# An encoder block with 32 experts: two more weight slots, sums over experts kept in PSUM, down biases added later, conditional loads on another queue

## The chip, the cores and the metric

The kernel runs on one core of a Trainium2 chip, as one launch. Times are device microseconds of that core. The kernel before ran three times: 1157.16, 1157.80 and 1158.95 us, median 1157.8 us. A further execution was taken with the profiler; its rows are what is read below.

## The reference, cut to what matters

One layer of an encoder over 256 tokens of width 1024, in float32. Two attention mixers (one that picks 64 keys per token with an indexer, one over chunks with a position bias) read one combined projection of x, are merged under gates, and are followed by a normalisation. Then comes a mixture of experts, and a second normalisation. Nearly all the data is in the experts: 32 of them, each with three matrices of 1024 x 1024.

```
x = layer_norm(DN_ALPHA * x + merged @ w_out, ln1_g, ln1_b)
logits = x @ w_router + b_router           # top 4 of 32, softmax over the four
for each expert e, for the tokens that take it:
    hg = min(xb @ w_gate[e] + b_gate[e], 7)
    hu = clip(xb @ w_up[e] + b_up[e], -7, 7)
    h  = (hu + 1) * hg * sigmoid(1.702 * hg)
    y  = (h @ w_down[e] + b_down[e]) * gate
ffn = sum over experts
x = layer_norm(DN_ALPHA * x + ffn, ln2_g, ln2_b)
```

## The kernel before, in words

**Slots.** Large data lies in a pool of NSLOT = 25 buffers ("slots") of 128 partitions x 8 KiB, 1 MiB each. All matrices are cut into chunks of one slot. `plan` puts them into one list in the order of their use: 24 chunks of the attention's matrices, then per expert eight chunks of gate and up and four of down, with gate and up of the next expert ahead of down of this one. `load_next` (line 83) takes the next chunk of the list into a slot; `pump(reserve)` repeats that while fewer than NSLOT - reserve slots are in use, counted as the program is written out. A load whose slot is still being read waits on its queue until the reader is done. `done` and `free` give slots back to the count. In the first stage `used()` calls `pump` with the reserves of the list RESERVE, 25 numbers written out by hand, so that slots remain for the halves into which ACT, DVE and POOL split the matrices (lines 175 and 180).

**Order.** The schedule is by hand: each engine and each queue runs its instructions in the order in which the program writes them. SP's queue issues the loads. It also issues the small ones, in the program's order: router weights and position bias (lines 392 to 394), x and the first norm's vectors (657, 658), gate and up biases (882, 883), down biases (900).

**Experts.** From about 221 us the loop over experts runs. For expert e, PE multiplies the gathered tokens (64 rows at most) with gate and up (`gate_up`, lines 759 and 761), ACT copies the products out of PSUM, then PE does the down product of expert e-1 (`down`, 793). At odd e it gathers the tokens of the next pair of experts by products with one-hot matrices (`dispatch`, 635) and turns the gates (744). Then `act_fn` turns the products of gate and up (776), and DVE and ACT compute h. At even e `combine` (808) spreads a pair's rows over the 256 tokens, into PSUM banks c0 and c1, and DVE adds these to the sum `acc`, a slot in SBUF (814). `acc` begins as ALPHA times x1 at expert 0.

**PSUM.** All tiles in PSUM come from one pool of eight banks (`bank`), reused as they are released. At the last expert four banks are opened as `sums`: eight instructions multiply `acc` with the identity into them (963), and the last pair's rows are added there (990), from where the second norm reads them.

**Down biases.** At expert 3 `down_biases` loads the 32 x 1024 table into a slot (900), multiplies it with the turned gates (908), and DVE adds the four results to `acc` (910). It also computes the largest count of tokens of an expert, `cnti`. The slot is kept until expert 20.

**Overflow.** At expert 20 `overflow` reads `cnti` into a register on each engine (831) and branches (832): if an expert has more than 64 tokens, a loop over all experts works off the rest, with loads by SP inside the block. With the inputs here the block is not run. The loads that `pump` issues after expert 19's down weights, in the call with e = 19, go out on POOL's queue in place of SP's.

Of the kernel before, what the change touches and what calls it, by code (L numbers as in the profile page):

```python
# [15 lines left out]
NT = 2  # L16
# [4 lines left out]
CAP = 64  # L21
TOPK = 64
# [6 lines left out]
NSLOT = 25  # L29
# [19 lines left out]
def body(nc, tc, slots, sm, psp, xT_d, x_d, w_g0, w_qi, w_in, ikgb_d, wuk_d,  # L49
# [4 lines left out]
    # ---------------------------------------------------------------- slots and loads  # L54
# [53 lines left out]
    def plan_d(e):  # L108
        if e < NE - 1:
            for c in range(4):  # L110
                plan(("d", e, c), wd_d[e, c])
            return
        # the last expert's by halves of the columns
        for c2 in range(2):
            for h in range(2):
                plan(("dl", h, c2), lambda t, h=h, c2=c2: [
                    (t[:, i * 1024:(i + 1) * 1024].rearrange("p (k f) -> p k f", k=2),
                     wd_d[e, 2 * c2 + i].rearrange("p (k f) -> p k f", k=2)[:, :, h * 512:(h + 1) * 512])
                    for i in range(2)])
# [7 lines left out]
    # ---------------------------------------------------------------- first loads  # L127
# [13 lines left out]
    # ---------------------------------------------------------------- constants and small loads  # L141
    ident = sm.tile([128, 128], F32, name="ident")
    make_identity(nc, ident)
    ikgb = sm.tile([128, 3], F32, name="ikgb")
    SP.dma_start(ikgb, ikgb_d)
# [9 lines left out]
    epst = sm.tile([128, 1], F32, name="epst")  # L155
# [14 lines left out]
    # ---------------------------------------------------------------- exact halves of float32 operands  # L170
# [6 lines left out]
    def split(t, hi, lo, rnd=acopy, sub=G):  # L177
        """hi = t rounded to float32r, lo = what is left of it"""
        rnd(hi.bitcast(F32R), t)
        sub.tensor_tensor(lo.bitcast(F32R), t, hi, op=ALU.subtract)  # L180

    # the matrices whose products run on halves, in the order of their use
# [4 lines left out]
    def ahead(n):  # L187
        """splits the first n chunks of that order"""
        for key in order[len(halves):n]:
            t = take(key)  # L190
            hi, lo = slot("hi"), slot("lo")
            sub = {"V": V, "G": G}[LO_ENGINE[len(halves)]]
            for h in range(2):
                cs = slice(h * 1024, (h + 1) * 1024)
                split(t[:, cs], hi[:, cs], lo[:, cs], sub=sub)
            halves.append((hi, lo))
            done(1)

    def part(i, which, k, per):
        """row block k of chunk i"""  # L200
        return halves[i][which].bitcast(F32R).rearrange("p (k c) -> p k c", k=per)[:, k, :]
# [5 lines left out]
    def used():  # L207
        """chunk done with"""
        free(2)
        pump(next(pumps))  # L210

    # ---------------------------------------------------------------- index queries, feature-major
# [6 lines left out]
    def warm(n):  # L219
        """keeps the tensor engine's clock up while it waits"""  # L220
        p = bank("warm")
        for _ in range(n):
            PE.matmul(p[:, 0:128], wt, wt, start=True, stop=True)
# [31 lines left out]
    def project(g, sink):  # L255
        """group g of the input projections, token-major"""
        ps = [bank("tm") for _ in range(NT)]
        for c in range(2):
            i = IN + 2 * g + c
            ahead(i + 1 + AHEAD[i])  # L260
            for tb in range(NT):
                for k in range(4):
                    for a, b in THREE:
                        PE.matmul(ps[tb], xHL[a][:, 4 * c + k, tb * 128:(tb + 1) * 128], part(i, b, k, 4),
                                  start=(c + k + a + b == 0), stop=(c == 1 and k == 3 and b == 1))
                if c == 1:
                    sink(tb, ps[tb])
            used()

    def project_T(g, sink):  # L270
        """group g of the input projections, feature-major; two row blocks share a bank, so only the first starts it"""
# [21 lines left out]
    # k_idx layer norm and c_kv rms norm, token-major  # L293
# [26 lines left out]
    def head_scores(qT, kT, tb, sink):  # L320
        """pairs of heads lie on the two halves of the partitions"""
# [14 lines left out]
    # ---------------------------------------------------------------- B queries and keys, the indexer  # L336
# [51 lines left out]
    # ---------------------------------------------------------------- A queries  # L388
# [8 lines left out]
    # ---------------------------------------------------------------- attention  # L397
# [91 lines left out]
    # ---------------------------------------------------------------- merge  # L489
# [21 lines left out]
    def branch(w, c, ps):  # L511
        """chunk c of a branch's rows; at the last one the gate and, for B, the sum of the two and its halves"""
# [36 lines left out]
    def norm_apply(tb, groups):  # L549
        """z = (x1 - mean) * rstd, and x1 = z * g + b"""  # L550
# [38 lines left out]
    def route_sums(copy=vcopy):  # L589
        """the router's products by experts, in four sums over two row blocks each"""  # L590
        p = bank("rt")
        for k in range(KD):
            g = k % 4
            PE.matmul(p[32 * g:32 * g + 32, 0:128], wrg[:, k, :], zT[:, k, :], start=(k < 4), stop=(k >= 4),
                      skip_group_check=True)
        copy(rsum, p[:, 0:128])

    def route(tb):
        """the router's logits (the norm's gain in the weights, its offset in the row), and which experts a token takes"""
# [9 lines left out]
    def count_up(tb):  # L609
        """the place of each token among an expert's tokens; far off for the tokens that it doesn't take"""  # L610
# [11 lines left out]
    sgm = wa_s[:, 1536:1792].rearrange("p (j s) -> p j s", j=4)  # L622

# [38 lines left out]
    # the second token tile's last columns in two halves, for a shorter way from their sums to the norm  # L662
# [66 lines left out]
    # ---------------------------------------------------------------- experts  # L729
# [9 lines left out]
    def combine_weights(pt, gated):  # L739
        """pt = the gated one-hot rows turned, from their two halves of 64 columns for each token tile"""  # L740
# [6 lines left out]
    def dispatch_weights(g):  # L747
        """for the pair g of experts"""
# [39 lines left out]
    def down(hT, wd):  # L788
        """the halves of the columns on the halves of the partitions"""
# [7 lines left out]
    def rows_of(e, p, first=0, size=512):  # L797
        """an expert's rows to its half of the pair's partitions"""
        r = slice(64 * (e % 2), 64 * (e % 2) + 64)
        for n in range(2):  # L800
            acopy(work["y"][r, first + n * size:first + (n + 1) * size], p[64 * n:64 * n + 64, 0:size])

    def combine(g):
        """adds a pair's rows to the sums"""
        for tb in range(NT):
            ps = [bank("c0"), bank("c1")]
            for n in range(2):
                PE.matmul(ps[n], work["pt"][:, g % 2, tb, :], work["y"][:, n * 512:(n + 1) * 512], start=True, stop=True)  # L808
            add(tb, ps)

    def add(tb, ps):
        for n in range(2):
            cs = slice(n * 512, (n + 1) * 512)
            V.tensor_tensor(acc[:, tb, cs], acc[:, tb, cs], ps[n], op=ALU.add)
# [8 lines left out]
    def overflow(s):  # L823
# [8 lines left out]
        with tc.If(rv > CAP):  # L832
            for r in range(1, T // CAP):
                with tc.For_i(0, NE, 1) as e:
# [18 lines left out]
                    def stream(src):  # L853
                        def get(j, cs):
                            o = (j % 2) * 1024
                            SP.dma_start(ow, src[col, j // 2, :, o + cs.start:o + cs.stop]
# [9 lines left out]
                    for tb in range(NT):  # L866
                        cps = [bank("c0"), bank("c1")]
                        for n in range(2):
                            h = slice(64 * n, 64 * n + 64)
                            PE.matmul(cps[n], opt[h, tb, :], y[h, :], start=True, stop=True)  # L870
                        add(tb, cps)
# [23 lines left out]
    def down_biases():  # L895
        """the gates' share of the down biases; the largest count of an expert's tokens"""
        bd_s = slot("bd")
        gT = bd_s[0:NE, 1024:1024 + T]
        bd = bd_s[0:NE, 0:1024]
        SP.dma_start(bd, bd_d)  # L900
# [4 lines left out]
        for tb in range(NT):  # L905
            for n in range(2):
                p = bank("bd")
                PE.matmul(p, gT[:, tb * 128:(tb + 1) * 128], bd[:, n * 512:(n + 1) * 512], start=True, stop=True)
                cs = slice(n * 512, (n + 1) * 512)
                V.tensor_tensor(acc[:, tb, cs], acc[:, tb, cs], p, op=ALU.add)  # L910
# [5 lines left out]
        return bd_s  # L916
# [6 lines left out]
    def run_down(e):  # L923
        p = down(work["hT"], wchunks("d", e))
        done(4)
        pump(0, G if e == 19 else SP)
        rows_of(e, p)

    acc = None
    last = NE - 1  # L930
    for e in range(last):
        ps = run_gate_up(e)
        if e == 0:
            open_work()
            acc_s = slot("acc")
            acc = acc_s.rearrange("p (b c) -> p b c", b=2)
            gates()
        evac_gu(ps)
        if e == 0:
            V.tensor_scalar(acc_s, x1_s, ALPHA, None, op0=ALU.mult)  # L940
        if e == 1:
            dispatch_weights(0)
        if e == 3:
            ov_s = down_biases()
# [10 lines left out]
        if e == 20:  # L955
            overflow(ov_s)
            free()

    # the last expert: the sums move to PSUM
    sums = [[bank("sum") for _ in range(2)] for _ in range(NT)]  # L960
    for tb in range(NT):
        for n in range(2):
            PE.matmul(sums[tb][n], ident, acc[:, tb, n * 512:(n + 1) * 512], start=True, stop=False,  # L963
                      skip_group_check=True)
# [4 lines left out]
    ln2_s = slot("ln2")  # L969
# [4 lines left out]
    # ---------------------------------------------------------------- last expert's end, second norm  # L974
# [111 lines left out]
```

## Time and profile before

| what | value |
|---|---|
| median of three runs | 1157.8 us |
| the profiled execution's span, first to last instruction | 1156.1 us |
| its mean granted TensorE clock | 0.975 |
| PE busy | 1067.6 us, 92% |
| DVE, ACT, POOL busy | 351.9, 227.6, 85.5 us |
| moved by DMA | 437.51 MB, mean 378 GB/s |

The profiled execution's own time beside its span is not recorded; the span is what there is. Busy times are of one engine each, and engines overlap. PE is TensorE's matrix products, PEld its weight loads, DVE, ACT, POOL and SP the other engines; a name with a q is the engine's sequencer, which waits, branches and issues transfers. In the row of 40 slices one slice is 28.9 us. L759 is line 759 of the kernel; a line of a helper (83, 175, 180) serves many callers.

### The profile page before, as it was taken

How to read it: one execution, taken by the hardware profiler on the slowest of the kernel's cores; microseconds unless marked ns; L12 is line 12 of the kernel's file. 1: busy time of each engine (PE TensorE's matmuls, PEld its weight loads, DVE VectorE, ACT ScalarE, POOL GpSimd, SP SyncE). 2: the span in 40 equal slices, each digit the busy share in tenths (PEclk: the TensorE clock that was granted, in tenths of full speed). 3: DMA queues.
4: the chain of work that ended last, by engine and by line, in shares of the span. 5: the costliest groups of instructions: out<-in, count | busy, mean ns of one | idle time of the engine just before them, and what ended most of it. 6: DMA issues, size and time to landing. Idle time of an engine off the chain costs nothing. (4 is left out here: it accounts for less than half of the span.)

```text
span 1156.1 us, 13824 instructions
## 1 busy us (share of the span) xinstructions
PE 1067.6 (92%) x5599; PEld 540.9 (47%) x5599; DVE 351.9 (30%) x811; ACT 227.6 (20%) x424; POOL 85.5 (7%) x60
## 2 busy tenths in 40 slices
PE   8997899999899999999899999996699999999896
PEld 8987899634244443434343434341243434343432
DVE  6797826412212322121212121210212121212124
ACT  3645342221011111111111111110011111111112
POOL 4113723000000000000000000001000000000001
PEclk9997999999899999999999999998799999999998
DMA  8940747999999999999999999999989999999995
GB/s 335 382 154 1 280 180 306 359 420 422 407 405 421 421 420 421 421 421 421 421 421 421 421 422 421 421 422 422 418 353 421 421 421 421 421 421 421 421 421 189
DMA packets 63932, 437.51 MB, mean 378 GB/s; under 512 B 7252, under 2 KB 7892, under 8 KB 11892
## 3 DMA queue, kind: packets, MB, share of 16 engines
q1 hardware_dynamic: 61270, 421.61, 88.5%
q0 software_dynamic: 1728, 12.58, 2.6%
q10 hardware_dynamic: 864, 2.36, 0.6%
q8 instruction: 46, 0.75, 0.3%
q14 instruction: 24, 0.20, 0.0%
HBM read 435.48 MB, written 1.05 MB: 378 GB/s over the span
## 5 line engine op out<-in xcount | busy, mean ns | idle before, releaser
L761 PE MATMUL gu<-ld,wa 128*64 128x512 f32 x1024 | 458.9, 602 | 27.3 <-DMA ld<-in_dram 23.4
L759 PE MATMUL gu<-ld,wa 128*64 128x512 f32 x1024 | 457.9, 601 | 7.5 <-DVEq L832 6.8
L793 PE MATMUL y<-ld,wc 128*64 128x512 f32 x992 | 240.4, 606 | 19.7 <-DMA ld<-in_dram 19.7
L759 PEld LDWEIGHTS gu<-ld,wa 128*64 128x64 f32 x1024 | 136.7, 138 | 241.0 <-issue 221.4
L780 DVE TENSOR_TENSOR wc<-tr,wb 128x256 f32<-128x256 f32 x64 | 27.0, 422 | 669.7 <-PE tr L776 669.7
L761 PEld LDWEIGHTS gu<-ld,wa 128*64 128x64 f32 x1024 | 136.2, 138 | 93.2 <-DMA ld<-in_dram 46.4
L793 PEld LDWEIGHTS y<-ld,wc 128*64 128x64 f32 x992 | 77.4, 138 | 169.6 <-issue 131.2
L175 ACT ACTIVATE wb<-gu 128x512 f32<-128x512 f32 x64 | 38.3, 598 | 442.6 <-PE gu L761 234.5
L175 ACT ACTIVATE wc<-y 64x512 f32<-64x512 f32 (+1 forms) x66 | 38.3, 580 | 239.8 <-PE y L793 234.1
L279 PE MATMUL fm<-xh,hi 128*128 128x256 f32 x224 | 66.4, 297 | 9.7 <-ACT sa_vb L175 5.4
L635 PEld LDWEIGHTS ga<-wa,x 128*128 128x128 f32 x512 | 61.6, 196 | 12.4 <-issue 12.2
L180 POOL TENSOR_TENSOR lo<-ld,hi 128x1024 fp32r<-128x1024 f32 x24 | 59.0, 2491 | 97.7 <-ACT hi L175 72.4
L279 PE MATMUL fm<-xl,hi 128*128 128x256 f32 x224 | 65.2, 291 | 0.0
L279 PE MATMUL fm<-xh,lo 128*128 128x256 f32 x224 | 65.1, 291 | 0.0
L635 PE MATMUL ga<-wa,x 128*128 128x128 f32 x512 | 64.8, 285 | 0.0
L808 PE MATMUL c<-wc,wb 128*128 128x512 f32 x120 | 54.0, 592 | 0.0
L83 POOL DMA_DIRECT2D ld<-in_dram x12 | 6.7, 558 | 608.8 <-DMA ld<-in_dram 578.1
L175 ACT ACTIVATE hi<-ld 128x1024 fp32r<-128x1024 f32 x48 | 47.1, 1048 | 17.6 <-PE fm L279 8.8
L279 PEld LDWEIGHTS fm<-xh,hi 128*128 128x128 f32 x224 | 45.0, 201 | 10.9 <-ACT sa_vb L175 5.8
L279 PEld LDWEIGHTS fm<-xl,hi 128*128 128x128 f32 x224 | 45.0, 201 | 0.2 <-issue 0.2
L279 PEld LDWEIGHTS fm<-xh,lo 128*128 128x128 f32 x224 | 44.9, 200 | 0.0
L180 DVE TENSOR_TENSOR lo<-ld,hi 128x1024 fp32r<-128x1024 f32 x24 | 33.8, 1461 | 30.2 <-ACT hi L175 27.4
(244 smaller groups left out, 882.0 us busy)
## 6 DMA issues: line engine op xcount, KB each, us to landing
ld<-in_dram SPq DMA_DIRECT2D x392, 1024.0 KB, 19.8
ld<-in_dram POOLq DMA_DIRECT2D x12, 1024.0 KB, 25.0
ld<-in_dram SPq DMA_DIRECT2D x8, 512.0 KB, 14.2
wq<-in_dram ACTq DMA_DIRECT2D x3, 512.0 KB, 8.7
biasB<-in_dram SPq DMA_DIRECT2D x1, 1024.0 KB
x<-in_dram SPq DMA_DIRECT2D x1, 1024.0 KB
g<-in_dram SPq DMA_DIRECT2D x1, 800.0 KB, 9.7
xT<-in_dram SPq DMA_DIRECT2D x3, 256.0 KB, 6.9
```

The costliest lines, as they stand in the source:

```text
L83: eng.dma_start(part, from_)
L175: A.activation(o, i, AF.Copy)
L180: sub.tensor_tensor(lo.bitcast(F32R), t, hi, op=ALU.subtract)
L279: PE.matmul(ps[j // 2][:, j % 2 * 256:j % 2 * 256 + 256], part(i, b, k, 4)[:, j * 128:(j + 1) * 128], xHL[a][:, 4 * c + k, :], start=(c + ...
L635: PE.matmul(ps[j // per][:, (j % per) * n:(j % per + 1) * n], x1_cols(tb, j), Pt, start=(tb == 0 and j % per == 0), stop=(tb == 1), skip_g ...
L759: PE.matmul(ps[n][0:64, :], xe(j), wg(j, cs), start=(j == 0), stop=(j == KD - 1), skip_group_check=True)
L761: PE.matmul(ps[n][64:128, :], xe(j), wu(j, cs), start=(j == 0), stop=(j == KD - 1), skip_group_check=True)
L780: V.tensor_tensor(gg, pv[:, :, 0, :], bg(js), op=ALU.add)
L793: PE.matmul(p[64 * n:64 * n + 64, :], hT[:, j, :], wd(j, slice(n * 512, (n + 1) * 512)), start=(j == 0), stop=(j == KD - 1), skip_group_ch ...
L808: PE.matmul(ps[n], work["pt"][:, g % 2, tb, :], work["y"][:, n * 512:(n + 1) * 512], start=True, stop=True)
```

## The change

- NSLOT goes from 25 to 27. The list of reserves stays. To make room, a small tile (`epst`) becomes a column of another, and the scratch memory for descriptors of POOL's transfers is set to 1024 (last line).
- `sums` is opened ahead of the expert loop and holds four of the eight banks until the end. At expert 0 `open_sums` multiplies x1 with ALPHA times the identity into them; every `combine`, and the overflow block, adds to them on PE. The slot `acc` is taken only at the end, for the second norm's results; the adds on DVE go.
- The largest count stays at expert 3 (`count`). The down biases are loaded after expert 26 and multiplied after expert 28, into `sums`.
- The overflow block's loads go out on POOL's queue; the block's slot is taken at expert 20 alone. All `pump` loads go out on SP's queue. One slot is kept free by four calls of `pump`, for the overflow block and for the biases.
- Comments are dropped.

```
+OVERFLOW_AT = 20
+BD_AT = 26
-NSLOT = 25
+NSLOT = 27
-    ikgb = sm.tile([128, 3], F32, name="ikgb")
-    SP.dma_start(ikgb, ikgb_d)
+    ikgb = sm.tile([128, 4], F32, name="ikgb")
+    SP.dma_start(ikgb[:, 0:3], ikgb_d)
-    epst = sm.tile([128, 1], F32, name="epst")
+    epst = ikgb[:, 3:4]
+    identa = wa_s[:, 1792:1920]
+    def summed(tb, n, lhsT, rhs, start=False, stop=False):
+        PE.matmul(sums[tb][n], lhsT, rhs, start=start, stop=stop, skip_group_check=True)
+    def open_sums():
+        V.tensor_scalar(identa, ident, ALPHA, None, op0=ALU.mult)
+        for tb in range(NT):
+            for n in range(2):
+                summed(tb, n, identa, x1[:, tb, n * 512:(n + 1) * 512], start=True)
     def combine(g):
         for tb in range(NT):
-            ps = [bank("c0"), bank("c1")]
             for n in range(2):
-                PE.matmul(ps[n], work["pt"][:, g % 2, tb, :], work["y"][:, n * 512:(n + 1) * 512], start=True, stop=True)
-            add(tb, ps)
+                summed(tb, n, work["pt"][:, g % 2, tb, :], work["y"][:, n * 512:(n + 1) * 512])
...
-                            SP.dma_start(ow, src[col, j // 2, :, o + cs.start:o + cs.stop]
+                            G.dma_start(ow, src[col, j // 2, :, o + cs.start:o + cs.stop]
...
-    def down_biases():
-        bd_s = slot("bd")
+    def down_biases(bd_s):
...
-        SP.dma_start(bd, bd_d)
...
-                p = bank("bd")
-                PE.matmul(p, gT[:, tb * 128:(tb + 1) * 128], bd[:, n * 512:(n + 1) * 512], start=True, stop=True)
-                cs = slice(n * 512, (n + 1) * 512)
-                V.tensor_tensor(acc[:, tb, cs], acc[:, tb, cs], p, op=ALU.add)
+                summed(tb, n, gT[:, tb * 128:(tb + 1) * 128], bd[:, n * 512:(n + 1) * 512])
+    def count():
         p = bank("cnt")
...
-        pump(0, G if e == 19 else SP)
+        pump(1 if e in (OVERFLOW_AT - 2, OVERFLOW_AT - 1, BD_AT - 2, BD_AT - 1) else 0)
         rows_of(e, p)
+    sums = [[bank("sum") for _ in range(2)] for _ in range(NT)]
...
-            acc_s = slot("acc")
-            acc = acc_s.rearrange("p (b c) -> p b c", b=2)
...
-            V.tensor_scalar(acc_s, x1_s, ALPHA, None, op0=ALU.mult)
+            open_sums()
...
-            ov_s = down_biases()
+            count()
...
-        if e == 20:
-            overflow(ov_s)
+        if e == OVERFLOW_AT:
+            overflow(slot("ov"))
             free()
-    sums = [[bank("sum") for _ in range(2)] for _ in range(NT)]
-    for tb in range(NT):
-        for n in range(2):
-            PE.matmul(sums[tb][n], ident, acc[:, tb, n * 512:(n + 1) * 512], start=True, stop=False,
-                      skip_group_check=True)
+        if e == BD_AT:
+            bd_s = slot("bd")
+            SP.dma_start(bd_s[0:NE, 0:1024], bd_d)
+        if e == BD_AT + 2:
+            down_biases(bd_s)
+            free()
...
-    nc = _bacc.Bacc("TRN2", target_bir_lowering=False, num_devices=1)
+    nc = _bacc.Bacc("TRN2", target_bir_lowering=False, num_devices=1, dynamic_dma_scratch_size=1024)
```

## Rows read from the trace of the kernel before

**Rows 1.** The page: span; busy tenths of PE and GB/s in 40 slices.
```profile
span 1156.1 us, 13824 instructions
...
PE   8997899999899999999899999996699999999896
...
GB/s 335 382 154 1 280 180 306 359 420 422 407 405 421 421 420 421 421 421 421 421 421 421 421 422 421 421 422 422 418 353 421 421 421 421 421 421 421 421 421 189
```

**Rows 2.** Stretches: us, busy of PE, PEld, DVE, ACT, POOL; granted clock; DMA share; GB/s.
```profile
0.00:205.00 205.00, 187.60 (x1425) 176.09 (x1426) 141.97 (x247) 90.62 (x162) 73.67 (x45) 0.96 0.60 234
...
225.00:235.00 10.00, 10.00 (x49) 3.18 (x46) 1.37 (x2) 0.60 (x1) 0.00 (x0) 1.00 0.93 359
...
300.00:335.00 35.00, 31.57 (x136) 13.65 (x134) 8.12 (x22) 4.94 (x10) 0.00 (x0) 0.85 0.99 394
...
540.00:780.00 240.00, 218.48 (x1002) 90.61 (x1000) 47.23 (x128) 31.62 (x60) 1.40 (x2) 1.00 1.01 421
...
835.00:850.00 15.00, 11.12 (x44) 3.54 (x42) 0.00 (x0) 1.20 (x2) 0.00 (x0) 0.89 0.72 287
...
1130.00:1141.00 11.00, 10.93 (x79) 5.49 (x76) 1.23 (x4) 3.49 (x6) 2.29 (x1) 1.00 0.82 301
```

**Rows 3.** Waits of SP's queue: us in total, times, longest us.
```profile
SPq L83 <- DMA ld<-in_dram: 598.8, 285, 4.6
...
SPq L83 <- DVE lo L180: 45.1, 6, 16.1
SPq L832 <- SPq L832: 36.9, 6, 13.6
```

**Rows 4.** Transfers by issuing line: count, KB each, median us to landing.
```profile
ld<-in_dram SPq DMA_DIRECT2D x392, 1024.0 KB, 19.8
```

**Rows 5.** Chain that ended last, from 1100 us: start us, us, what.
```profile
1102.30 0.69 PE tr L776 x4
...
1106.08 0.34 DVE wc L783
...
1108.38 3.70 PE sum L963 x8
...
1128.29 11.35 DMA ld<-in_dram
```

**Rows 6.** Instructions on the bias tables: duration ns min/median/max, first and last start.
```profile
L394 SPq DMA_DIRECT2D biasB<-in_dram x1: 328/328/328, 59.0 to 59.0; - x1
L399 DVE MEMSET biasB<- x1: 485/485/485, 73.5 to 73.5; 64x512 f32 x1
...
DMA to landing us min/median/max: 6.2/6.2/6.2
```

**Rows 7.** Chain that ended last, from 856 us.
```profile
856.02 3.97 PE ga L635 x32
...
860.20 0.96 PE tr L776 x8
...
875.04 6.87 PE y L793 x32
...
883.07 3.44 PE c L808 x8
```

**Rows 8.** Groups by line and shape: busy us, mean ns, idle before and releaser.
```profile
L175 ACT ACTIVATE wa<-ga 128x512 f32<-128x512 f32 x32 | 19.1, 598 | 33.8 <-PE ga L635 33.8
...
L175 ACT ACTIVATE wb<-ptx 128x256 f32<-128x256 f32 x16 | 6.1, 379 | 0.0
```

**Rows 9.** Instructions on the down biases' tile, and what they waited for.
```profile
L908 PE MATMUL bd<-bd x8: 1056/1056/1185, 305.8 to 311.9; 32*128 32x512 f32 x8
...
  DMA bd<-in_dram: 3.4, 1
```

**Rows 10.** Instructions of line 832, the branch at expert 20.
```profile
L832 SPq EVENT_SEMAPHORE  x8: 17/17/17, 820.5 to 844.0; - x8
...
L832 POOLq COMPARE_BRANCH  x1: 45/45/45, 815.0 to 815.0; - x1
```

More of the change, by code (lines that the diff above doesn't have):

```diff
@@ L801, in rows_of @@
             acopy(work["y"][r, first + n * size:first + (n + 1) * size], p[64 * n:64 * n + 64, 0:size])
+    def summed(tb, n, lhsT, rhs, start=False, stop=False):
[5 more added lines that the diff above has]
+                summed(tb, n, identa, x1[:, tb, n * 512:(n + 1) * 512], start=True)
     def combine(g):
         for tb in range(NT):
-            ps = [bank("c0"), bank("c1")]
             for n in range(2):
-                PE.matmul(ps[n], work["pt"][:, g % 2, tb, :], work["y"][:, n * 512:(n + 1) * 512], start=True, stop=True)
-            add(tb, ps)
-    def add(tb, ps):
-        for n in range(2):
-            cs = slice(n * 512, (n + 1) * 512)
-            V.tensor_tensor(acc[:, tb, cs], acc[:, tb, cs], ps[n], op=ALU.add)
+                summed(tb, n, work["pt"][:, g % 2, tb, :], work["y"][:, n * 512:(n + 1) * 512])
     def wchunks(kind, e):
@@ L866, in overflow @@
                     for tb in range(NT):
-                        cps = [bank("c0"), bank("c1")]
                         for n in range(2):
                             h = slice(64 * n, 64 * n + 64)
-                            PE.matmul(cps[n], opt[h, tb, :], y[h, :], start=True, stop=True)
-                        add(tb, cps)
+                            summed(tb, n, opt[h, tb, :], y[h, :])
     def open_work():
@@ L906, in down_biases @@
             for n in range(2):
-                p = bank("bd")
-                PE.matmul(p, gT[:, tb * 128:(tb + 1) * 128], bd[:, n * 512:(n + 1) * 512], start=True, stop=True)
-                cs = slice(n * 512, (n + 1) * 512)
-                V.tensor_tensor(acc[:, tb, cs], acc[:, tb, cs], p, op=ALU.add)
+                summed(tb, n, gT[:, tb * 128:(tb + 1) * 128], bd[:, n * 512:(n + 1) * 512])
+    def count():
         p = bank("cnt")
@@ L915, in down_biases @@
         V.tensor_copy(cnti, cnt)
-        return bd_s
     def run_gate_up(e):
@@ L925, in run_down @@
         done(4)
-        pump(0, G if e == 19 else SP)
+        pump(1 if e in (OVERFLOW_AT - 2, OVERFLOW_AT - 1, BD_AT - 2, BD_AT - 1) else 0)
         rows_of(e, p)
-    acc = None
+    sums = [[bank("sum") for _ in range(2)] for _ in range(NT)]
     last = NE - 1
@@ L954, in body @@
             combine(e // 2 - 1)
-        if e == 20:
-            overflow(ov_s)
+        if e == OVERFLOW_AT:
+            overflow(slot("ov"))
             free()
-    sums = [[bank("sum") for _ in range(2)] for _ in range(NT)]
-    for tb in range(NT):
-        for n in range(2):
-            PE.matmul(sums[tb][n], ident, acc[:, tb, n * 512:(n + 1) * 512], start=True, stop=False,
-                      skip_group_check=True)
+        if e == BD_AT:
[4 more added lines that the diff above has]
+            free()
     evac_gu(run_gate_up(last))
@@ L968, in body @@
     run_down(last - 1)
-    ln2_s = slot("ln2")
+    ln2_s, acc_s = slot("ln2"), slot("acc")
+    acc = acc_s.rearrange("p (b c) -> p b c", b=2)
     SP.dma_start(ln2_s[0:1, :], ln2_d)
```

## The prediction

> **What bounds the kernel now.** I read the page's slices first. From about 230 us to 1130 us the PE row stands mostly at 9 and the GB/s row at about 421, with one drop to 353 [rows 1]; two rows that are both full don't say who waits. The stretches do [rows 2]: from 540 to 780 us PE is busy 218.5 of 240 us, while the DMA engines are full (share 1.01) at 421 GB/s. So the transfers set the pace and PE follows. The waits of SP agree: 285 times, 598.8 us in all, it stood before its next load until an earlier one landed [rows 3]. A load of 1 MiB takes 19.8 us to land [rows 4]; at 421 GB/s one costs 1.0486 MB / 421 = 2.49 us, so eight are in flight. The chain near the end is DMA too: 11.35 us of it up to 1139.6 us, and only then the last products and the norm [rows 5].
>
> The bytes don't change, so the time can change only where the DMA engines stand still or the tail after the last load does. Time lost against 421 GB/s is width x (421 - rate)/421 [rows 2]: 0 to 205 us, 234 GB/s: 91.1 us. 225 to 235, 359: 1.5. 300 to 335, 394: 2.2. 540 to 780: nothing. 835 to 850, 287: 4.8. After 1141 us come the 15.1 us of the tail.
>
> **The change part by part, two more slots.** In the first 205 us SP waits for slots: 45.1 us for DVE's low halves alone [rows 3]. The count along the program, with the same reserves and 27 slots, has every refill end two chunks further on: 18 loads rather than 16 ahead of the small loads of line 392, 31 rather than 29 after group 6, 49 rather than 47 ahead of expert 0. Two chunks of 2.49 us have room many times over in the 91.1 us lost, so when the engines become full two loads are done that were not: **5.0 us**. From below: 0, if slots come free in an order that makes SP stand where it did not. From above: 5.0 plus the 1.5 lost at 225 to 235 us. I take 5.0, since those two loads need no buffer's release, and the stop at 225 comes from a wait for gate/up's first weights that stays.
>
> The two loads are now in front of the bias tables on SP's queue. The last of those tables was issued at 59.0 us and took 6.2 us, so it was there at 65.2; DVE first touches them at 73.5 [rows 6]. A delay of 5.0 us fits into these 8.3 us; without that cover it would be paid in full.
>
> **The sums in PSUM.** Before, the slot of acc was held from expert 0 on and that of the down biases from 3 to 20; now neither is, so weights have 23 slots in place of 19 or 20 (22 while one is kept for the overflow or the biases). The 60 adds on DVE go: nothing, since DVE is off the path, used 47.2 of 240 us in the steady stretch [rows 2]. The eight matmuls that open the sums, 3.70 us [rows 5], move from expert 31 to expert 0. At either place PE does not set the end: for a pair of experts PE needs 2 x 13.88 (gate/up, 861.16 to 875.04 us) + 2 x 6.87 (down) + 3.97 (gather) + 0.21 (gates, up to 860.20) + 0.96 and 1.16 (the turnings, the second from 881.91 to 883.07) + 3.44 (combine) = 51.24 us [rows 7], the transfers 24 x 2.49 = 59.8, so 8.5 us per pair are free. Were PE the bound there, the move would cost 3.7.
>
> Four banks are left to turn over where eight were. Walking the order (gate/up two, down one, gather two, gates one, turning two), each new tile finds the bank used four tiles before. The one late release that I find is after a gather: gate/up's second bank is that of the gates, which ACT copies behind two copies of the gathered rows, 2 x 0.598 + 0.379 = 1.58 us [rows 8], while PE needs 0.21 + 0.96 = 1.17 [rows 7]: 0.4 us per pair, inside the 8.5. Bounds: 0 to the 7.2 us of the slower rival below.
>
> **The down biases, late.** At expert 3 PE sits 3.4 us waiting for that table, its eight matmuls then last 1.056 us each [rows 9], and the granted clock of 300 to 335 us is 0.85 [rows 2], part of it at the lower level of 1.2 GHz; PE then gives slots back late, and the transfers lose the 2.2 us. Now the load is issued two experts before its use and the eight matmuls stand at expert 28. Their price there is about that of the other eight, 3.7 us, inside a pair's 8.5. With three or four more slots and no stop, I take the whole **2.2 us**; from below 0, if the dip comes from the slots being short anyhow.
>
> **Overflow on POOL's queue.** At expert 20 every engine branches around a block that isn't run. SP, whose loads stand in the block, has eight semaphore records there, 820.5 to 844.0 us [rows 10], and stands 36.9 us [rows 3]: as I read it, it waits until each of its loads in flight has landed and only then issues again. POOL's twelve loads after expert 19's down product cover this, and when they too have landed the engines run dry: the 4.8 us. POOL, which branches too but issues nothing in the block, has one branch and nothing behind it [rows 10]. The change swaps the roles. SP then passes like POOL, with up to 19.8 us of loads in flight, and the twelve loads return to SP, whose queue waits 598.8 us for landings anyway. POOL waits for its own loads, of which there are none. I take **4.8 us**; bounds 0 (SP still drains, without POOL's cover) and 4.8.
>
> Shrinking the descriptor scratch and moving the epsilon into another tile cost nothing: POOL no longer issues a transfer that runs, and the memset and the load write different columns.
>
> **Sum.** 5.0 + 2.2 + 4.8 = 12.0 us. The profiled execution is known by its span, 1156.1 us [rows 1]; the median of the runs is 1157.8, so 1.7 us lie around it, left as they are. 1156.1 - 12.0 = 1144.1 of span, 1145.8 of time.
>
> The Trainium skill (DMA: Bandwidth & Descriptors, Where 436 GB/s comes from) says that a load from HBM is bound at about 358 GB/s per core. The trace differs: 421 over 240 us [rows 2], and the trace decides. By the page, 394 GB/s would be no dip, a chunk would cost 2.93 us, and 835 to 850 us would lose 3.0: 5.9 + 3.0 = 8.9 us, 1148.9; with 240 us against it I give that no chance of its own.
>
> **The rivals.** *SP still stands in the block, or the two early loads gain nothing.* Either leaves about 4.8 or 5.0 us: a gain of 7.1, 1150.7. For it: SP's longest gap in the block is 13.6 us [rows 3], and I can't say that all of it is landings. Against: POOL's single record.
>
> *More than counted.* The 1.5 us at 225 to 235 us vanish as well, and as much again of the small losses around it: 1142.8. For it: a third slot is free from expert 0 on. Against: in that stretch SP waits for the first gate/up weights to be used.
>
> *No change.* The end is paced by PE after all, which from 1130 to 1141 us is busy 10.9 of 11 us [rows 2]: within 2 us of 1157.8. Against: the chain has the last load, not PE, end last there, and the opening matmuls, 3.7 us, leave that very place [rows 5].
>
> *Slower: four banks.* If gate/up gets the bank that the turning has just filled, it waits for DVE to read it, from 1103.0 to 1106.4 us in the chain [rows 5]: 3.4 us per expert, with the 0.4 above 7.2 per pair. PE's expert stage begins at about 221 us, and some 15 us follow the last load, so PE alone would end at 221 + 16 x (51.2 + s) + 15 = 1055 + 16 s. It overtakes the transfers at s = 5.6 and is slower than before from s = 6.3; at 7.2 the span is 1170, the time 1172. Against: expert 31 already ran with four banks held, and gate/up, turning and down follow each other there.
>
> **How the numbers follow.** About 0.2% can be told from no change, 2.3 us. Main case 0.68: 1145.8, its own range 1143.5 to 1149. One of the two large terms missing 0.14: 1150.7. More 0.05: 1142.8. No change 0.05. Slower 0.08. Faster is 0.68 + 0.14 + 0.05 = 0.87. The range reaches from 1142.5 over the case with one term missing to 1151.5, and leaves out 0.13 and some edges.
>
> **What would show it.** Right: 49 loads issued ahead of expert 0; 421 GB/s from 235 us to the last load, without the dips at 300 and 840; no semaphore records of SP at line 832; the last load landing near 1129 us with a tail of 15. Wrong: SP's queue waiting at the branch and a dip near expert 20; PE idle in gate/up behind DVE or ACT; PE busy throughout beyond 600 us; or a first stage longer than 221 us.

## The result, and the profile after

| kernel | median | runs | ratio to before, 95% interval |
|---|---|---|---|
| before | 1157.84 us | 4 | |
| changed | 1148.73 us (1147.88 to 1151.11) | 4 | 0.9924 [0.9908, 0.9939] |

The change makes the kernel 9.1 us faster; 12.0 had been forecast, and 1148.73 lies inside the range. The profiled execution of the changed kernel is its slowest run, 1151.11 us with a span of 1149.5, so 1.6 us lie around the span. The same kernel was timed twice more as a mark for the experiments: 1148.65 us, ratio 0.9918 [0.9906, 0.9931], and 1148.82 us, ratio 0.9926 [0.9912, 0.9939].

The page of the changed kernel, as in [rows 1] (one of 40 slices is 28.7 us):

```profile
span 1149.5 us, 13751 instructions
...
PE   8996899999999999999999999997999999989996
...
GB/s 359 397 182 13 251 178 341 341 398 422 421 420 422 420 421 422 421 421 421 421 421 421 419 422 420 422 421 420 420 420 422 420 423 421 421 405 422 420 414 158
```

The drop to 353 is gone, and so are the 407 and 405 near 300 us. There is a 398 in the ninth slice, and a new 405 near 1020 us. Of the kernel before, two stretches that [rows 2] does not have, and then the stretches of the changed kernel (columns as in [rows 2]):

```profile
235.00:260.00 25.00, 24.95 (x126) 10.28 (x127) 5.61 (x18) 5.38 (x9) 0.00 (x0) 1.00 1.01 422
...
1000.00:1060.00 60.00, 54.98 (x255) 22.95 (x253) 11.81 (x32) 7.91 (x15) 0.00 (x0) 1.00 1.01 421
```

```profile
0.00:205.00 205.00, 187.56 (x1407) 176.21 (x1408) 141.23 (x245) 90.42 (x162) 73.70 (x45) 0.96 0.62 242
225.00:235.00 10.00, 10.00 (x50) 3.37 (x48) 1.10 (x8) 0.32 (x1) 0.00 (x0) 1.00 1.02 416
235.00:260.00 25.00, 25.00 (x112) 9.17 (x110) 5.61 (x18) 4.78 (x8) 0.00 (x0) 1.00 0.97 398
300.00:335.00 35.00, 35.00 (x184) 14.73 (x181) 5.45 (x18) 5.88 (x11) 0.00 (x0) 1.00 1.01 420
540.00:780.00 240.00, 218.75 (x1002) 89.00 (x1000) 37.67 (x112) 31.55 (x60) 0.00 (x0) 1.00 1.01 421
835.00:850.00 15.00, 15.00 (x74) 5.48 (x74) 4.30 (x12) 2.21 (x6) 0.00 (x0) 1.00 1.01 419
1000.00:1060.00 60.00, 55.69 (x254) 23.77 (x252) 9.42 (x28) 8.26 (x16) 0.00 (x0) 1.00 1.01 413
1130.00:1141.00 11.00, 8.37 (x42) 3.30 (x40) 3.91 (x8) 1.80 (x5) 1.46 (x1) 1.00 0.08 31
```

In the steady stretch nothing has changed: PE is busy 218.75 of 240 us (218.48 before), the engines are full at 421 GB/s. Two stretches carry a loss that the kernel before did not have. From 235 to 260 us it is 25 x (421 - 398)/421 = 1.4 us (422 GB/s before), and from 1000 to 1060 us 60 x (421 - 413)/421 = 1.1 us (421 before).

SP's waits, and the branch (line 832 before, 838 now), beside [rows 3] and [rows 10]. SP no longer waits at the branch, where it stood 36.9 us in all, and its waits for landings rise from 598.8 to 685.8 us:

```profile
SPq L85 <- DMA ld<-in_dram: 685.8, 329, 3.6
...
SPq L85 <- DVE lo L182: 44.9, 5, 16.2
```

```profile
L838 POOLq COMPARE_BRANCH  x1: 45/45/45, 307.6 to 307.6; - x1
...
L838 SPq COMPARE_BRANCH  x1: 50/50/50, 829.2 to 829.2; - x1
```

SP has one branch record and no semaphore records at line 838; its loads on either side of the branch are issued at 827.92 and 830.42 us, the usual 2.5 us apart. POOL, which has nothing in flight, comes to the branch already at expert 3 (307.6 us); its four semaphore records of line 838 lie within 0.3 us at 313 us.

The chain that ended last, from 1122 us (start us, us, what), beside [rows 5]:

```profile
1122.14 10.78 DMA ld<-in_dram
...
1132.96 1.08 PE y L983 x8
1134.05 1.05 PE sum L990 x2
1135.10 1.01 PE y L983 x8
1136.12 2.00 PE sum L990 x4
```

The last landing on record, that of load 411 of 412, is at 1132.9 us; 16.6 us of tail follow (16.5 before). The chain runs from that landing into the last products without a wait for anything else, so it is still the transfers that set the end.

**Where along the program the time was gained.** Whatever paces the kernel, PE uses the loads in their order, so the landing of the same load in two traces shows what was gained up to there. The table gives it for three profiled executions of the changed kernel, as differences to the one of before (loads counted from 1, landing times of before at the head; load 372 has no landing on record in these four traces, so it is that of 371 plus 2.49 us).

```
load                52     60    140    260    320    372    411
before, us       243.9  264.2  466.7  766.5  920.0 1049.4 1139.6
after             -4.4   -2.4   -4.6   -4.7   -7.7   -6.5   -6.7
after_again       -4.6   -2.7   -5.0   -4.9   -7.8   -6.7   -7.7
after_third       -6.1   -4.6   -6.9   -7.0   -9.9   -8.8   -8.9
```

The starts of the three differ by up to 1.7 us, but the steps between the columns agree: 4.4 to 6.1 us won up to load 52, 1.5 to 2.0 given back between loads 52 and 60, 2.2 to 2.3 won up to load 140, nothing up to 260, 2.9 to 3.0 won at the branch, and then 1.1 to 1.2 given back between loads 320 and 372. The experiments ask what stands behind each.

### The profile page after: what moved, and what is told of

The parts are those of the page before. It is cut to its first block, busy times and chain, and to the rows that moved or that the text cites. A ratio compares the mean times of both kernels' runs of the same rounds, so it can differ in the third digit from the quotient of the medians.

```text
span 1149.5 us, 13751 instructions
## 1 busy us (share of the span) xinstructions
PE 1065.6 (93%) x5599; PEld 544.8 (47%) x5599; DVE 313.1 (27%) x747; ACT 227.3 (20%) x424; POOL 78.8 (7%) x48
## 4 chain that ended last, share of the span: by engine, by line
DMA 61%; PE 31%; DVE 7%; issue 1%; SPq 0%; ACT 0%; POOL 0%; DVEq 0%; ACTq 0%
DMA ld<-in_dram 60%; PE gu L762 10%; PE fm L281 5%; PE y L796 4%; PE br L518 2%; PE wo L652 2%; PE sum L808 2%; PE ga L638 1%; DVE biasB L416 1%; DVE sa_vb L416 1%; DMA wq<-in_dram 1%; PE tr L779 1%; PE gu L764 1%; DVE misc L385 1%; DVE misc L363 1%
## 5 line engine op out<-in xcount | busy, mean ns | idle before, releaser
L762 PEld LDWEIGHTS gu<-ld,wa 128*64 128x64 f32 x1024 | 135.1, 137 | 208.5 <-issue 203.3
L764 PEld LDWEIGHTS gu<-ld,wa 128*64 128x64 f32 x1024 | 134.6, 137 | 126.4 <-issue 64.1
L796 PEld LDWEIGHTS y<-ld,wc 128*64 128x64 f32 x992 | 80.1, 136 | 164.6 <-issue 118.8
L971 POOL PARTITION_BROADCAST ln<-ln x1 | 2.3, 2297 | 928.0 <-DMA ld<-in_dram 928.0
L808 PE MATMUL sum<-wc,wb 128*128 128x512 f32 x120 | 54.0, 593 | 0.0
L177 ACT ACTIVATE hi<-ld 128x1024 fp32r<-128x1024 f32 x48 | 46.9, 1046 | 16.6 <-PE fm L281 8.8
L785 ACT ACTIVATE wa<-wc 128x256 f32<-128x256 f32 x64 | 26.7, 416 | 79.7 <-DVE wc L784 77.5
## 6 DMA issues: line engine op xcount, KB each, us to landing
ld<-in_dram SPq DMA_DIRECT2D x404, 1024.0 KB, 19.8
```

The costliest lines, as they stand in the source:

```text
L177: A.activation(o, i, AF.Copy)
L762: PE.matmul(ps[n][0:64, :], xe(j), wg(j, cs), start=(j == 0), stop=(j == KD - 1), skip_group_check=True)
L764: PE.matmul(ps[n][64:128, :], xe(j), wu(j, cs), start=(j == 0), stop=(j == KD - 1), skip_group_check=True)
L785: A.activation(sg_, gg, AF.Sigmoid, scale=1.702)
L796: PE.matmul(p[64 * n:64 * n + 64, :], hT[:, j, :], wd(j, slice(n * 512, (n + 1) * 512)), start=(j == 0), stop=(j == KD - 1), skip_group_ch ...
L808: PE.matmul(sums[tb][n], lhsT, rhs, start=start, stop=stop, skip_group_check=True)
```

## Experiments

The theory at the outset: three causes, each on its own, two earlier loads, the biases' place, and the branch. A rival for each was that the part does nothing and another one has its gain. The first series undoes one part of the changed kernel at a time (before: 1157.65 us, 11 runs).

**The mark.** The changed kernel itself.

> The changed kernel itself, with more rounds. Theory A (the forecast's mechanisms, each a little smaller): the gain over the kernel before stays near 9 us, 1148 to 1149.5. Rival: the 12.0 us of the forecast were there and the first runs were slow ones: 1146. In its profile theory A expects again: SP passes the branch at expert 20 within about 1 us, and a dip of 1 to 2 us in the transfers near 245 us.

Measured: 1148.65 us (1147.79 to 1150.15). Theory A holds, and the rival of 1146 us falls: SP has no semaphore records at the branch, and 235 to 260 us run at 403 GB/s, a loss of 1.1 us.

**Slots back.**

```
-NSLOT = 27
+NSLOT = 25
```

> The changed kernel with 25 slots in place of 27, all else as changed. Theory A: two chunks less are loaded ahead of expert 0, 2 x 2.49 us: 5.0 us slower than the changed kernel, about 1153.7. Rival: slots were not what the first stage lacked, and the third slot (the one of the sum that is no longer held) is enough: within 1 us of the changed kernel.

Measured: 1152.70 us (1151.36 to 1155.46), ratio 0.9964 [0.9952, 0.9977]. That is 4.0 us above the mark by the medians; by the ratios 0.0046 x 1157.65 = 5.3. The two slots are worth 4 to 5 us. The rival (within 1 us of the changed kernel) falls. In its trace load 52 lands 2.8 us earlier than before, where the changed kernel has 4.4 to 6.1: 1.6 to 3.3 us apart. The profiled executions account for the rest of the 4 to 5 us: that of this kernel lies 1.3 us under its median, and those of the changed kernel 1.3 us over theirs on average.

**Overflow loads back on SP.** The twelve covering loads on POOL stay away.

```
-   G.dma_start(ow, src[col, j // 2, :, ...
+   SP.dma_start(ow, src[col, j // 2, :, ...
```

> The changed kernel with the overflow block's loads on SP's queue again, without the twelve loads on POOL's queue that stood beside them before. Theory A: SP waits at the branch until its loads in flight have landed, the DMA engines run dry once, 4 to 6 us: about 1153. Rival 1: without POOL's cover PE runs out of weights as well and more is lost: 1156 to 1160. Rival 2: eight loads in flight and 27 slots cover the wait: within 1 us of the changed kernel. The profile should show semaphore records of SP at the branch and a dip near 800 to 850 us.

Measured: 1152.78 us (1150.20 to 1155.43), ratio 0.9949 [0.9936, 0.9962]: 4.1 us above the mark (3.6 by the ratios). Three views of this kernel, the instructions of line 838, SP's waits and the stretch 835 to 850 us:

```profile
L838 SPq EVENT_SEMAPHORE  x8: 17/17/17, 840.0 to 847.7; - x8
```

```profile
SPq L838 <- SPq L838: 18.5, 4, 11.1
```

```profile
835.00:850.00 15.00, 15.00 (x74) 5.01 (x72) 3.47 (x10) 1.95 (x4) 0.00 (x0) 1.00 0.57 224
```

Two neighbouring loads on SP are issued at 827.66 and 847.87 us, 20.2 us apart, which is the time of one load from issue to landing (19.8). So a queue that issues inside the block does wait at the branch until its last load has landed, although the block is not run; with POOL as the issuer that costs SP nothing. The prediction's rival, that SP stands there in the changed kernel too, falls.

**Biases back at expert 3**, load and products; no slot is kept free for them at experts 24 and 25.

```
-        pump(1 if e in (OVERFLOW_AT - 2, OVERFLOW_AT - 1, BD_AT - 2, BD_AT - 1) else 0)
+        pump(1 if e in (OVERFLOW_AT - 2, OVERFLOW_AT - 1) else 0)
...
         if e == 3:
+            bd_s = slot("bd")
+            SP.dma_start(bd_s[0:NE, 0:1024], bd_d)
+            down_biases(bd_s)
+            free()
...
-        if e == BD_AT: ...
-        if e == BD_AT + 2: ...
```

> The changed kernel with the down biases loaded and multiplied at expert 3, where the kernel before has them, into the sums in PSUM. Theory A: PE stands behind that load again, its clock falls, and transfers dip by up to 2.2 us around 300 to 340 us: 1150 to 1151. Rival: with 23 slots for weights the stop of PE is covered and moving the biases was worth nothing: within 1 us of the changed kernel, or up to 1 us faster, since the table's load then costs less there.

Measured: 1149.13 us (1145.94 to 1151.93), ratio 0.9922 [0.9908, 0.9937], 0.5 us above the mark: no difference that can be told, so by the time the rival holds. Its stretches 300 to 345 and 1000 to 1060 us say why:

```profile
300.00:345.00 45.00, 40.48 (x174) 16.49 (x172) 5.46 (x18) 5.54 (x11) 0.00 (x0) 0.85 1.00 402
1000.00:1060.00 60.00, 55.02 (x255) 22.37 (x252) 9.42 (x28) 7.89 (x15) 0.00 (x0) 1.00 1.01 421
```

At expert 3 the loss is 45 x 19/421 = 2.0 us, with more free slots than before, so the dip does come from the biases. But the 1.1 us at 1009 to 1028 us are gone. The move doesn't remove a loss of 2 us, it exchanges it for one of 1.1.

The second series (before: 1158.14 us, 15 runs) tried the one part that had been costed at nothing, and the two new drops.

**The sums alone.** The kernel before with `sums` opened at expert 0 and nothing else of the change; the diff, cut, is against the changed kernel.

```
-NSLOT = 27
+NSLOT = 25
...
-        pump(1 if e in (...) else 0)
+        pump(0, G if e == 19 else SP)
(biases at expert 3, their slot kept for the overflow at 20, whose loads are SP's; descriptor scratch as before)
```

> The kernel before with one part of the change alone: the sums over the experts lie in four PSUM banks from expert 0 on, and the slot of acc and the 60 adds on VectorE are gone. 25 slots, the down biases at expert 3 and in the slot that waits for the overflow, overflow loads on SP and the twelve covering loads on POOL at expert 19 are as before. Theory (the parts add up: slots about 4 to 5 us, the swap of queues about 4, the biases' place 0 to 0.5): nothing is left for the sums, 1156.5 to 1158.5 us, ratio 0.999 to 1.001, and the drops at 300 to 335 and 835 to 850 us stay. Rival: the freed slot of acc and the idle VectorE earn part of the 9 us by themselves: 1155 or less. Second rival: the four banks cost something that the other parts cover: 1160 or more.

Measured: 1157.14 us (1155.60 to 1159.63, 11 runs), ratio 0.9999 [0.9989, 1.0008]. Four banks, 60 adds less and a freed slot change nothing that can be told. Its trace shows two small effects that cancel:

```profile
225.00:235.00 10.00, 10.00 (x45) 3.41 (x42) 0.00 (x0) 1.66 (x3) 0.00 (x0) 1.00 1.01 412
235.00:260.00 25.00, 25.00 (x115) 9.16 (x114) 5.60 (x18) 3.38 (x7) 0.00 (x0) 1.00 0.97 400
```

At 225 to 235 us, where the kernel before has 359 GB/s, 10 x (412 - 359)/421 = 1.3 us are won, where the freed slot of `acc` comes in, and 25 x 21/421 = 1.2 us are lost just behind, where the sums are opened. (The landings say 1.1 us won between loads 46 and 52 and 0.8 lost up to load 60.) So the parts add up: 4.0 for the slots, 4.1 for the queues, 0.5 for the biases' place, 0 to 1.0 for the sums, together 8.6 to 9.6, with 9.1 measured for all; each of the parts is uncertain by 1 us or more.

**Without the table's load.**

```
-            SP.dma_start(bd_s[0:NE, 0:1024], bd_d)
+            V.memset(bd_s[0:NE, 0:1024], 0.0)
```

> The changed kernel without the load of the down biases' table (128 KiB on 32 partitions, issued by SP at expert 26); VectorE writes zeros into its place, the products at expert 28 stay. It leaves the down biases out of the sum. Theory (the table's load displaces other transfers and costs about 1.1 us wherever it stands; this is what ate half of the forecast 2.2): 1147.0 to 1148.0 us, and 1000 to 1050 us at 420 GB/s in place of 412. Rival (the load is hidden, and its transfer of 0.13 MB costs 0.3 us): the drop at 1009 us stays, 1148.3 to 1149 us.

Measured: 1147.40 us (1145.41 to 1149.21), ratio 0.9908 [0.9892, 0.9925]. The time alone would not decide it; the stretch does:

```profile
1000.00:1060.00 60.00, 56.84 (x254) 22.71 (x252) 9.40 (x28) 8.26 (x16) 0.00 (x0) 0.97 1.01 421
```

The drop is gone with the load, and load 372 lands as far ahead as load 320 does (8.6 and 8.5 us). A load of 128 KiB, worth 0.31 us by its bytes, costs 1.1.

**Sums opened at expert 2** in place of 0.

```
-        if e == 0:
-            open_sums()
...
         act_fn(work["hT"], bias_of(0, e), bias_of(1, e))
+        if e == 2:
+            open_sums()
         if e >= 2 and e % 2 == 0:
             combine(e // 2 - 1)
```

> The changed kernel with the eight matmuls that open the sums moved from expert 0 to expert 2, ahead of the first pair's combine. Theory (at expert 0 their 3.7 us on PE give slots back late when all slots wait, and this is the new drop to about 303 GB/s at 245 to 250 us): the drop is gone, 1.0 to 1.5 us less, 1147.2 to 1147.8 us. Rival (the drop comes from the first experts' other work on PE and ACT, the gather and the gates, and the matmuls only stand beside it): the drop stays and the time is 1148.3 to 1149.2 us; or it only moves to expert 2, with the same time.

Measured: 1147.14 us (1145.02 to 1147.63), ratio 0.9908 [0.9893, 0.9922]. The interval meets the mark's ([0.9906, 0.9931]), so the time does not decide. The drop at 241 to 251 us is gone, so it did come from the eight matmuls. But one has come at 301 to 306 us, 45 x 10/421 = 1.1 us, as the last of the rivals has it. The stretches of this kernel from 235 to 345 us, and the lines of the tile `sum` there:

```profile
235.00:260.00 25.00, 25.00 (x130) 10.53 (x130) 5.18 (x18) 4.65 (x9) 0.00 (x0) 1.00 1.01 422
260.00:300.00 40.00, 35.45 (x145) 14.18 (x146) 8.73 (x25) 5.18 (x11) 0.00 (x0) 0.91 1.01 421
300.00:345.00 45.00, 45.00 (x230) 17.93 (x226) 5.45 (x18) 5.87 (x11) 0.00 (x0) 1.00 0.99 411
...
288.00:294.30 6.30, 6.08 (x8) 2.65 (x9) 0.07 (x1) 0.00 (x0) 0.00 (x0) 0.52 1.01 420
```

```profile
L808 PE MATMUL sum<-x,wa x8: 593/1061/1191, 288.2 to 294.2; 128*128 128x512 f32 x8
...
  DVE wa L811: 4.6, 1
```

PE stood 4.6 us until DVE had made the scaled identity, which `open_sums` orders only there, and then ran most of the eight matmuls in about 1061 ns where 592 is usual, at the lower of the two levels, 1.2 GHz: 0.52 was granted from 288.0 to 294.3 us.

**Both moves together:** sums opened at expert 2, biases at expert 3.

> The changed kernel with the sums opened at expert 2 and the down biases loaded and multiplied at expert 3, so that nothing of either is left at experts 0, 26 and 28. Theory (each of the two small drops is a loss of its own, and the dip at expert 3 is the table's load and a late slot, as dear as the one at expert 26): as open2, 1147.2 to 1148.2 us. Rival (with the opening out of the way the third free slot covers expert 3, and both losses go): 1146.0 to 1147.0 us. Second rival (opening and biases close together make one longer dip): 1149 us or more.

Measured: 1148.10 us (1146.56 to 1149.48), ratio 0.9923 [0.9910, 0.9937]. Its 300 to 345 us run at 405 GB/s, a loss of 1.7; the rest up to 1060 us is full. That is the first expectation, at its upper end.

The third series (before: 1157.59 us, 10 runs) repeats the mark and the opening at expert 2 on one chip, and takes away the stall that this had brought.

> The changed kernel itself, as the mark for the three kernels timed beside it on the same chip: 1148 to 1149.5 us, with the drop at 241 to 251 us and the one at 1018 to 1028 us.

Measured: 1148.82 us (1147.41 to 1150.37).

> The kernel with the sums opened at expert 2, again, beside the changed one. Its trace showed the drop of 1.45 us at 241 to 251 us gone and one of 1.15 us at 301 to 306 us come, so the theory now is that the move is worth 0.3 us and the 1.5 us between the medians were chance: ratio to the changed kernel of the same call 0.999 to 1.0005. Rival: it is faster by 1 us or more here too.

Measured: 1147.66 us (1145.63 to 1149.88), ratio 0.9917 [0.9902, 0.9932], 0.9991 of the mark: inside the theory's range (0.999 to 1.0005), but 1.0 to 1.2 us faster, which is the rival's condition too, so the time does not part them. Its stretch 300 to 345 us has 415 GB/s: 0.6 us are lost there, in place of the 1.4 us that the mark loses at 235 to 260 us. So the loss was moved and, here, became 0.8 us smaller; that the 1.5 us of the series before was chance is not shown.

**The identity made in time.** The sums are opened at expert 2, as in the one before.

```
...
         if e == 0:
             open_work()
             gates()
+            V.tensor_scalar(identa, ident, ALPHA, None, op0=ALU.mult)
...
 def open_sums():
-    V.tensor_scalar(identa, ident, ALPHA, None, op0=ALU.mult)
```

> As the one before, but the scaled identity that opens the sums is made at expert 0. At expert 2 TensorE stood 4.6 us for it and then ran the eight matmuls at the lower clock (1061 ns for one, where 592 ns is the usual). Theory (that stall and the slow matmuls make the slots late and cause the drop at 301 us): the drop goes, and the time is 1.0 to 1.5 us under the changed kernel. Rival (the drop at 301 us has another cause, or any wait of TensorE there turns into one somewhere): a drop of about 1 us stays between 235 and 345 us, and the time is within 0.5 us of the kernel opened at expert 2.

Measured: 1145.37 us (1145.08 to 1148.82), ratio 0.9897 [0.9883, 0.9912], the lowest of all kernels; its interval meets that of the mark (from 0.9912) at one end, so it is faster than the kernel before, and very likely than the changed one. By the medians that is 3.4 us, more than the 1.0 to 1.5 expected; the drop explains 1.4, and what the rest is, if it isn't chance, no stretch shows. Its stretches:

```profile
235.00:260.00 25.00, 24.95 (x121) 9.25 (x118) 5.60 (x18) 5.72 (x10) 0.00 (x0) 1.00 1.01 423
260.00:300.00 40.00, 40.00 (x190) 17.16 (x190) 8.61 (x24) 5.75 (x12) 0.00 (x0) 1.00 1.01 422
300.00:345.00 45.00, 45.00 (x224) 18.90 (x222) 9.47 (x30) 7.90 (x15) 0.00 (x0) 1.00 1.01 421
```

No drop is left between 235 and 345 us. The rival (some drop stays) falls. Loads 52 and 60 land 4.5 and 4.6 us earlier than before: the 1.5 to 2.0 us that the changed kernel gives back between them are kept.

**The table on ScalarE's queue**, on top of that.

```
-            SP.dma_start(bd_s[0:NE, 0:1024], bd_d)
+            A.dma_start(bd_s[0:NE, 0:1024], bd_d)
```

> As the one before, and the table of the down biases is issued on ScalarE's queue in place of SP's. On SP's queue it cost 1.1 us of transfer, although its bytes are worth 0.13 MB / 421 = 0.31 us. Theory (the table takes one of the eight places in SP's queue, and with only seven weight loads behind it some engines run dry): on another queue the loss shrinks to 0.3 us, 0.8 us less than the one before. Rival (the table's rows go unevenly to the engines, whoever issues it): 1.1 us are lost about its landing as before.

Measured: 1146.51 us (1145.58 to 1148.18), ratio 0.9905 [0.9891, 0.9920]; against the one before no difference that can be told. The table's own line, and the stretch:

```profile
L959 ACTq DMA_DIRECT2D bd<-in_dram x1: 349/349/349, 1006.6 to 1006.6; - x1
...
DMA to landing us min/median/max: 5.6/5.6/5.6
```

```profile
1000.00:1060.00 60.00, 53.73 (x230) 22.87 (x228) 9.41 (x28) 8.05 (x17) 0.00 (x0) 0.89 1.01 418
```

It lands after 5.6 us in place of 18.9 and costs 60 x 3/421 = 0.4 us, near the 0.3 of its bytes. With the table on SP's queue the same stretch has 415 GB/s in the kernel just before this one (0.9 us) and 413 to 414 in the changed one (1.0 to 1.1). So about half of the cost or more is a matter of the queue, not of the table. That the eight places in SP's queue are the reason fits, but another reason within that queue was not excluded.

## Why the prediction was right, and where it was off

**What bounds the kernel** held: full engines at 421 GB/s, a tail of 16.6 us behind the last load, and PE with slack in the steady stretch. Of the signs that were named, two came: 49 loads are issued ahead of the small ones of expert 0 (line 886), and SP has no semaphore records at the branch. Two did not: the dips near 300 and 840 us are gone, but the engines are not full all the way from 235 us, and the last landing on record is at 1132.9 us, not near 1129. The rival of the four banks falls: `sums_only` holds them and costs nothing that can be told, and PE's busy time in 540 to 780 us is what it was. The rival that PE paces the end falls with the chain.

**Two more slots, 5.0:** right in mechanism and size: the slots alone are worth 4.0 to 5.3 by the times. Not all of the 4.4 to 6.1 us at load 52 is theirs. Between loads 46 and 52 the changed kernel wins 0.8 to 1.2 us over the one before, and `slots25` and `sums_only`, with 25 slots, win 1.1 there too; so this piece goes with the sums and the slot of `acc` that they free, as the rival *more than counted* had it for the 1.5 us at 225 to 235 us. The main case did not count it. The last bias table's load is issued at 60.0 us in place of 59.0, so of the feared delay of 5.0 us only 1.0 came.

**The down biases late, 2.2:** right at expert 3 (2.2 to 2.3 us between loads 60 and 140), but the other end of the move was costed only in PE's time. The load two experts ahead of its use was taken as free; in a queue that is never dry it costs 1.1 us. Net, undoing the move changes 0.5 us, which can't be told from nothing.

**The sums in PSUM, 0:** this is the step of the working that failed. It said of the eight opening matmuls that "at either place PE does not set the end", and showed it with the balance of a pair of experts: 8.5 us free. That balance belongs to the steady stretch. At expert 0 every slot that SP wants next is one that PE has yet to read; SP's waits in the changed kernel from 230 to 262 us are led by gate and up:

```profile
SPq L85 <- PE gu L764: 17.6, 5, 7.8
```

There 3.7 us more on PE (236.2 to 239.9 us) delay the slots, the engines run down to 398 GB/s, and 1.5 to 2.0 us of landing are lost. `open2` and `open2_early` show that the loss goes away with the matmuls, comes back at expert 2 where PE stalls, and is gone for good without that stall.

**Overflow on POOL's queue, 4.8:** the mechanism was right, and so was the size in bytes. The stretch 780 to 870 us before, in the changed kernel and in `ov_sp`:

```profile
780.00:870.00 90.00, 67.36 (x264) 24.51 (x262) 11.90 (x32) 7.90 (x15) 5.29 (x10) 0.87 0.96 399
```

```profile
780.00:870.00 90.00, 80.26 (x356) 35.80 (x356) 14.71 (x44) 11.09 (x21) 0.00 (x0) 0.94 1.01 420
```

```profile
780.00:870.00 90.00, 80.43 (x354) 30.42 (x350) 14.71 (x44) 11.10 (x21) 0.00 (x0) 0.94 0.94 388
```

The losses are 4.7, 0.2 and 7.1 us, so 4.5 us of bytes are won. In landings the part is worth less: 2.9 to 3.0 us between loads 260 and 320, and `ov_sp`, which misses 7.1 us of bytes, falls only 2.5 us behind the changed kernel there (its lead over before goes from 3.4 to 3.8 us). Its times say 3.6 to 4.1. The traces show where the difference lies. Between the landings of loads 260 and 320 the engines moved 63.3 MB in the changed kernel, 62.6 MB before and 61.5 MB in `ov_sp`, where sixty loads are 62.9 MB: after a stop, less of the loads that come later has been moved by the time a given load lands. The 0.7 MB are 1.7 us at 421 GB/s, and the 1.8 MB are 4.3 us, about what the landings lose less than the bytes. Counted by landings, then, a stop costs less than its bytes. Why a load lands later against its bytes where nothing stopped the engines, no run here shows.

Summed along the landings of the three traces: 4.4 to 6.1 (forecast 5.0), -1.5 to -2.0 (forecast 0), 2.2 to 2.3 (2.2), 2.9 to 3.0 (4.8), -1.1 to -1.2 for the table (0), and 0.1 to 0.9 on the rest: 6.7, 7.7 and 8.9. The forecast was 12.0, the medians give 9.1. The two costs set at nothing come to some 2.9 us and the branch to 1.9 less than forecast; against these 4.8 stand the small gains elsewhere and the 1.3 us by which the three profiled executions (1151.11, 1150.15 and 1148.95 us) lie on average above the medians of their kernel. The measured time is nearer to 1150.7, the rival with one large term missing, than to the main case's 1145.8; but no term is missing, several fell short. That 1148.9, the prediction's sum by a rate that its own trace contradicts, comes nearest of all is chance: the changed kernel runs at 421 GB/s too.

## What to carry to other kernels

Slack of an engine holds only in the stretch in which it was measured: where work is moved, look at what the queue waits for at the new place. A small load in a queue that is always full cost more than its bytes here, and less on a second queue that stood idle, though the time was too coarse to tell the two apart. And a drop in bandwidth that an edit removes should be looked for again further on, at the place where the edit has put the work.

## What the runs showed of the hardware

A queue with transfers inside a conditional block that is not run stood 18.5 us at the branch, until its last load had landed, and issued two neighbouring loads 20.2 us apart (`ov_sp`); at the same branch without such transfers they were 2.5 us apart. The table of 128 KiB took 18.9 us to land behind SP's loads and 5.6 us on ScalarE's queue, at a cost of 0.9 to 1.1 and 0.4 us of the engines' time. Right behind a wait of 4.6 us, TensorE had 0.52 of its clock granted for 6.3 us and took 1061 ns for a matmul that took 592 ns otherwise (`open2`). The Trainium skill (DMA: Bandwidth & Descriptors, Queues, rings and completion order) says that each DMA engine takes turns between the queues that have work for it, packet by packet; the trace agrees that queues take turns, with 5.6 against 18.9 us for a transfer that did not have to wait for what SP had put ahead of it, and does not show the packets.
